# Staggered start addresses for the split activation tiles of a two-layer decoder trunk

## The chip, the cores and the metric

The kernel runs on one core of one Trainium2 chip. The metric is the device time of one launch in microseconds (us), median of the runs. A difference is told in us and in per cent of that median.

## What is computed

Two layers on 512 tokens of width 1024, in float32. Each is a mixer between an input and an output projection, then a LayerNorm of the residual and a gated addition of a per-layer embedding:

```python
def reference(x, p, ...):
    for i in range(DEPTH):                      # 2
        if i % 2 == 0:
            s = conv_gdn_mixer(x, w_in_even[j], ...)   # 1024 -> 8208, short conv and gated delta rule, 2048 -> 1024
        else:
            s = hgrn2_mixer(x, w_in_odd[j], ...)       # 1024 -> 8192, gated linear recurrence, 2048 -> 1024
        x = layer_norm(DEEPNORM_ALPHA * x + s, ln_g[i], ln_b[i])
        gate = jax.nn.sigmoid((x @ w_pl_gate[i]).astype(jnp.float32))
        x = x + ((p[i] @ w_pl[i]).astype(jnp.float32) * gate).astype(x.dtype)
    return x
```

Five large products make up most of the work: the two input projections, the two output projections and the gate products, all over 128-deep slices of the contraction.

## The kernel before, in words

**The split.** Every float32 operand of a large product is kept as two tiles of a rounded 32-bit type: a high half (`xh`, `yh`, `x1h`, `ph`, `whi`) and a low half (`xl`, `yl`, `x1l`, `pl`, `wlo`). ScalarE writes the high half (L104, L160), VectorE the low one (L105, L161). `mm3` (L107 to L114) then makes three matmuls of each 128-deep slice: high weight with high activation (L112), high weight with low activation (L113), low weight with high activation (L114). Transposes and the recurrences use plain float32 matmuls instead.

**The tiles.** The layer's input x, transposed, lies in 16 tiles of 128 partitions by 512 columns (2048 bytes in each partition): `xh0` to `xh7` and `xl0` to `xl7`, made in `load_x` from the pool `acts` and kept for both layers. The mixer's output lies in 32 such tiles, `yh0` to `yh15` and `yl0` to `yl15` (`open_y`, a pool at the right end of the memory). After the LayerNorm each half of the tokens has 16 tiles of 256 columns, `x1h` and `x1l` (`x1tiles`; the first half in the pool of the tail, the second in the pool of the gates). A weight chunk is one tile pair of 128 by 1024, eight slices of 128 columns (512 bytes) each, in three buffers (`chunk_tiles`).

**Where they begin.** Take the offset of a tile to be its start address in the partition, less the last multiple of 512. Before the change, every weight slice has offset 448, every `xh` and `xl` offset 0, every `yh`, `yl`, `x1h`, `x1l`, `ph` and `pl` offset 384, and nearly all other working tiles of the two layers offset 384 (a few of the odd layer 352). Three small tiles that nothing reads (`ytop`, `askew`, `sskew`) set these offsets. The small weights of the two gate columns, `wba_h` and `wba_l` (128 by 16 for each slice), begin at 448 and go on by 64 bytes from slice to slice.

**The order.** `proj` runs eight slices of one weight chunk against the eight `xh` and `xl` pairs: 24 matmuls of 512 columns into one accumulator. `out_proj` runs 16 slices against `yh` and `yl`, for four of the eight output blocks with 512 columns and for four with 256 columns, twice. `hgrn_values` (accumulator `pi`) has it the other way round: there slices of `xh` and `xl` are the stationary operand and the weight tiles the moving one, in 256 columns. The gate products (`product`, accumulator `pgate`) run 256 columns of `x1h` and `x1l`. Between slices `pump` lets the steps of the recurrences in, by counts written out at the top of the file (GD, HG, LN). All DMAs are issued from the SyncE queue.

In the profile a matmul row names output<-moving operand and weight: `pq<-xh,whi` streams `xh` through the array against `whi`.

Of the kernel before, what the change touches and what calls it, by code (L numbers as in the profile page):

```python
# [14 lines left out]
F32 = mybir.dt.float32  # L15
F32R = mybir.dt.float32r
# [6 lines left out]
P = 128  # L23
D = 1024
KD = D // P
S = 512
# [21 lines left out]
class K:  # L48
# [110 lines left out]
    def split_to(self, hi, lo, src):  # L159
        self.nc.scalar.copy(hi, src)  # L160
        self.nc.vector.tensor_tensor(lo, src, hi.bitcast(F32), op=SUB)  # L161


    def constants(self):
        nc, cp = self.nc, self.const
# [96 lines left out]
    def load_x(self, srcs):  # L262

        nc = self.nc
        self.xh = [self.acts.tile([P, S], F32R, name=f"xh{k}") for k in range(KD)]
        self.xl = [self.acts.tile([P, S], F32R, name=f"xl{k}") for k in range(KD)]
        chs = [self.chunk_tiles() for _ in srcs]
        with self.tc.tile_pool(name="xin", bufs=1, reuse_waits="tile") as xp:
            for k in range(KD):
                if k % 2 == 0:  # L270
                    self.chunk_part(chs[0], srcs[0], slice(k * P, (k + 2) * P))
                raw = xp.tile([P, S], F32, name=f"xraw{k}")
                nc.sync.dma_start(raw, self.a["xT"][:, k * S:(k + 1) * S])
                self.split_to(self.xh[k], self.xl[k], raw)
                if k % 2 == 0:
                    for ch, src in zip(chs[1:], srcs[1:]):
                        self.chunk_part(ch, src, slice(k * P, (k + 2) * P))
        pss = [self.acc("pqkv") for _ in srcs]
        for k in range(KD):
            for ps, (_, hi, lo) in zip(pss, chs):  # L280
                self.mm3(ps, [(hi[:, k, :], lo[:, k, :], self.xh[k], self.xl[k])], k == 0, k == KD - 1)
        self.pre = pss

    def open_y(self, layer):
        self.ystack = ExitStack()
        yp = self.ystack.enter_context(
            self.tc.tile_pool(name=f"y{layer}", bufs=1, side="right", reuse_waits="tile"))
        self.yh = [yp.tile([P, S], F32R, name=f"yh{k}") for k in range(2 * KD)]
        self.yl = [yp.tile([P, S], F32R, name=f"yl{k}") for k in range(2 * KD)]


    def gates(self, hp):
# [610 lines left out]
    def tail(self, layer, wout, last):  # L903
        nc, a = self.nc, self.a
        NH = 2
        HT = S // NH
        sm = self.smalls
        tp = self.tc.tile_pool
        with tp(name=f"tail{layer}", bufs=1, reuse_waits="tile") as lp, self.psum(f"pt{layer}") as self.ps:
# [38 lines left out]
                self.split_to(ph.rearrange("p a b -> p (a b)"), pl_.rearrange("p a b -> p (a b)"), praw)  # L948

            def x1tiles(pool, hf):  # L950
                return [(pool.tile([P, HT], F32R, name=f"x1h{hf}_{f}"),
                         pool.tile([P, HT], F32R, name=f"x1l{hf}_{f}")) for f in range(KD)]

            def norm_half(hf):
                hs = slice(hf * HT, (hf + 1) * HT)
# [28 lines left out]
            self.prio = PRIO  # L984
            load_p()
            x1[0] = x1tiles(lp, 0)
            self.start(0, norm_half(0))
            out_proj((5, 6, 7), HT, HT, held)
# [3 lines left out]
            self.ystack.close()  # L992
            with tp(name=f"gate{layer}", bufs=1, side="right", reuse_waits="tile") as gp:
                x1[1] = x1tiles(gp, 1)
                self.start(0, norm_half(1))

# [123 lines left out]
```

## Time and profile before

| | us |
|---|---|
| median of 3 runs | 1229.6 |
| lowest and highest of them | 1228.88, 1230.12 |
| the profiled execution's own time | 1228.3 |
| its span, first to last instruction | 1226.6 |
| TensorE busy in it | 1208.9 |
| VectorE, ScalarE, GpSimd busy | 805.9, 560.1, 45.9 |

The profile is of one execution. TensorE's busy time is the union of its matmuls' spans, and these overlap, since a matmul's record runs on until its last result is out. How fast a stretch of matmuls runs is therefore read from start to start, not from the length of a record: the start of the last of n+1 matmuls in a row less the start of the first, divided by n. This is called the pace below.

### The profile page before, as it was taken

The numbers are of one execution on the slowest core, as the hardware profiler recorded it, in microseconds if no ns is written. First come the engines' busy times: TensorE is split into PE (matmuls) and PEld (weight loads), VectorE is DVE, ScalarE is ACT, GpSimd is POOL, SyncE is SP. The second block draws the span as 40 slices with busy tenths as digits, with TensorE's granted clock in tenths as the row PEclk, the third lists the DMA queues.
The fourth block names the chain that finished last, engine by engine and source line by source line (L and its number), as shares of the span: only waits on it lengthen the run. The fifth ranks groups of instructions, "written<-read, shape, count | busy, mean of one in ns | idle before, by whom it ended". The sixth has DMA issues, their size and how long they took to land.

```text
span 1226.6 us, 23658 instructions
## 1 busy us (share of the span) xinstructions
PE 1208.9 (99%) x9590; PEld 1025.3 (84%) x9590; DVE 805.9 (66%) x1835; ACT 560.1 (46%) x1316; POOL 45.9 (4%) x75
## 2 busy tenths in 40 slices
PE   7999999999999999999999999999999999999998
PEld 5777878787787788898998888888888888889988
DVE  7678777776869754349856475665757575644884
ACT  5554645354545443237534444443535444433471
POOL 3000000000000000111000000000000000001100
PEclk9999999999999999999999999999999999999999
DMA  6223222232222223354442221222122222234432
GB/s 212 85 75 102 69 87 87 73 100 70 87 82 90 62 78 99 112 160 131 153 136 88 72 77 62 87 69 88 57 96 73 78 79 69 87 103 152 142 102 88
DMA packets 37309, 117.07 MB, mean 95 GB/s; under 512 B 4144, under 2 KB 8016, under 8 KB 37200
## 3 DMA queue, kind: packets, MB, share of 16 engines
q1 hardware_dynamic: 37200, 115.56, 29.5%
q8 instruction: 75, 1.23, 0.4%
q14 instruction: 34, 0.28, 0.1%
HBM read 111.32 MB, written 4.23 MB: 94 GB/s over the span
## 4 chain that ended last, share of the span: by engine, by line
PE 85%; DVE 9%; ACT 4%; issue 1%; DMA 0%; POOL 0%; SPq 0%; DVEq 0%; POOLq 0%; ACTq 0%
PE pz L112 5%; PE pz L113 5%; PE pz L114 5%; PE pout L112 4%; PE pout L114 4%; PE pout L113 4%; PE pqkv L113 3%; PE pqkv L114 3%; PE pqkv L112 3%; PE pf L112 3%; PE pq L112 2%; PE pf L114 2%; PE pf L113 2%; PE pq L114 2%; PE pq L113 2%; PE pgate L113 2%
## 5 line engine op out<-in xcount | busy, mean ns | idle before, releaser
L104 ACT CAST whi<-wraw 128x1024 fp32r<-128x1024 f32 (+1 forms) x196 | 200.7, 1024 | 335.5 <-PE pout L113 87.0
L105 DVE TENSOR_TENSOR wlo<-wraw,whi 128x1024 fp32r<-128x1024 f32 (+1 forms) x196 | 238.5, 1217 | 168.1 <-ACT whi L104 167.4
L112 PE MATMUL pout<-yh,whi 128*128 128x256 f32 (+1 forms) x384 | 122.7, 320 | 0.0
L114 PE MATMUL pout<-yh,wlo 128*128 128x256 f32 (+1 forms) x384 | 122.5, 319 | 0.0
L113 PE MATMUL pout<-yl,whi 128*128 128x256 f32 (+1 forms) x384 | 122.0, 318 | 0.0
L112 PE MATMUL pz<-xh,whi 128*128 128x512 f32 x256 | 104.1, 406 | 0.0
L114 PE MATMUL pz<-xh,wlo 128*128 128x512 f32 x256 | 101.1, 395 | 0.0
L113 PE MATMUL pz<-xl,whi 128*128 128x512 f32 x256 | 100.8, 394 | 0.0
L112 PE MATMUL pqkv<-xh,whi 128*128 128x512 f32 x192 | 79.7, 415 | 4.9 <-ACT xh L160 4.9
L114 PE MATMUL pqkv<-xh,wlo 128*128 128x512 f32 x192 | 77.8, 405 | 2.6 <-DVE wlo L105 2.6
L113 PE MATMUL pqkv<-xl,whi 128*128 128x512 f32 x192 | 78.9, 411 | 0.0
L112 PEld LDWEIGHTS pout<-yh,whi 128*128 128x128 f32 x384 | 72.6, 189 | 5.8
L114 PEld LDWEIGHTS pout<-yh,wlo 128*128 128x128 f32 x384 | 72.4, 188 | 5.6
L113 PEld LDWEIGHTS pout<-yl,whi 128*128 128x128 f32 x384 | 72.2, 188 | 5.6
L112 PE MATMUL pi<-whi,xh 128*128 128x256 f32 x256 | 72.6, 284 | 0.0
L113 PE MATMUL pi<-wlo,xh 128*128 128x256 f32 x256 | 72.0, 281 | 0.0
L113 PE MATMUL pgate<-x1l,whi 128*128 128x256 f32 x256 | 71.2, 280 | 0.4 <-DVE x1l L161 0.4
L114 PE MATMUL pi<-whi,xl 128*128 128x256 f32 x256 | 71.2, 278 | 0.0
L112 PE MATMUL pgate<-x1h,whi 128*128 128x256 f32 x256 | 70.7, 281 | 0.1
L114 PE MATMUL pgate<-x1h,wlo 128*128 128x256 f32 x256 | 70.7, 278 | 0.0
L114 PEld LDWEIGHTS pz<-xh,wlo 128*128 128x128 f32 x256 | 48.1, 188 | 10.4
L112 PEld LDWEIGHTS pz<-xh,whi 128*128 128x128 f32 x256 | 48.2, 188 | 9.6
(326 smaller groups left out, 2876.4 us busy)
## 6 DMA issues: line engine op xcount, KB each, us to landing
wraw<-in_we SPq DMA_DIRECT2D x62, 512.0 KB, 3.5
wraw<-in_wo SPq DMA_DIRECT2D x48, 512.0 KB, 3.5
wraw<-in_woe SPq DMA_DIRECT2D x21, 512.0 KB, 3.5
wraw<-in_woo SPq DMA_DIRECT2D x21, 512.0 KB, 3.4
wraw<-in_wg SPq DMA_DIRECT2D x16, 512.0 KB, 3.7
wraw<-in_wi SPq DMA_DIRECT2D x16, 512.0 KB, 3.5
gb<-drows SPq DMA_DIRECT2D x8, 512.0 KB, 3.8
xraw<-in_xT SPq DMA_DIRECT2D x8, 256.0 KB, 4.5
```

The lines of the kernel that those rows point to most:

```text
L104: nc.scalar.copy(hi, raw)
L105: nc.vector.tensor_tensor(lo, raw, hi.bitcast(F32), op=SUB)
L112: nc.tensor.matmul(ps, wh, xh, start=first and i == 0, stop=False)
L113: nc.tensor.matmul(ps, wh, xl, start=False, stop=False)
L114: nc.tensor.matmul(ps, wl, xh, start=False, stop=last and i == n - 1)
```

## The change

A helper `skewed` makes a list of tiles with a spacer of 16 floats (64 bytes) behind each, so that each tile of the list begins 64 bytes further within 512 than the one before. `load_x`, `open_y` and `x1tiles` take their high tiles from it, then a spacer of 8 floats (32 bytes), then their low tiles. Nothing writes or reads the spacers. The scratch that the program reserves for DMA descriptors made in software is halved, from 16384 to 8192 bytes in each partition, which makes room.

| tiles | offset before | offset after |
|---|---|---|
| weight slices `whi`, `wlo` | 448 | 448 |
| `xh0`, `xh1`, ... `xh7` | 0 | 0, 64, ... 448 |
| `xl0`, `xl1`, ... `xl7` | 0 | 32, 96, ... 480 |
| `yh0`, `yh1`, `yh2`, `yh3`, ... | 384 | 352, 416, 480, 32, ... |
| `yl0`, `yl1`, `yl2`, ... | 384 | 384, 448, 0, ... |
| `x1h` and `x1l`, first half | 384 | from 416 and from 448, by 64 |
| `x1h` and `x1l`, second half | 384 | from 352 and from 384, by 64 |
| `ph`, `pl` | 384 | 416 |
| other working tiles of the two layers | 384 (few 352) | 416 (few 384; some of the tail 448) |

No instruction is added, removed or moved: on each engine the built programs have the same operations on the same tiles in the same order, and each waits for the same semaphore values. The addresses alone differ.

```diff
+    def skewed(self, pool, n, names):
+
+        tiles = []
+        for name in names:
+            tiles.append(pool.tile([P, n], F32R, name=name))
+            pool.tile([P, 16], F32, name=name + "_s")
+        return tiles
...
-        self.xh = [self.acts.tile([P, S], F32R, name=f"xh{k}") for k in range(KD)]
-        self.xl = [self.acts.tile([P, S], F32R, name=f"xl{k}") for k in range(KD)]
+        self.xh = self.skewed(self.acts, S, [f"xh{k}" for k in range(KD)])
+        self.acts.tile([P, 8], F32, name="xskew")
+        self.xl = self.skewed(self.acts, S, [f"xl{k}" for k in range(KD)])
...
-        self.yh = [yp.tile([P, S], F32R, name=f"yh{k}") for k in range(2 * KD)]
-        self.yl = [yp.tile([P, S], F32R, name=f"yl{k}") for k in range(2 * KD)]
+        self.yh = self.skewed(yp, S, [f"yh{k}" for k in range(2 * KD)])
+        yp.tile([P, 8], F32, name="yskew")
+        self.yl = self.skewed(yp, S, [f"yl{k}" for k in range(2 * KD)])
...
-                return [(pool.tile([P, HT], F32R, name=f"x1h{hf}_{f}"),
-                         pool.tile([P, HT], F32R, name=f"x1l{hf}_{f}")) for f in range(KD)]
+                xh = self.skewed(pool, HT, [f"x1h{hf}_{f}" for f in range(KD)])
+                pool.tile([P, 8], F32, name=f"x1skew{hf}")
+                return list(zip(xh, self.skewed(pool, HT, [f"x1l{hf}_{f}" for f in range(KD)])))
...
-    nc = _bacc.Bacc("TRN2", target_bir_lowering=False, num_devices=1)
+    nc = _bacc.Bacc("TRN2", target_bir_lowering=False, num_devices=1, dynamic_dma_scratch_size=8192)
```

## Rows read from the trace of the kernel before

**Rows 1.** The page: TensorE's busy time, and the chain that ended last.
```profile
PE 1208.9 (99%) x9590; PEld 1025.3 (84%) x9590; DVE 805.9 (66%) x1835; ACT 560.1 (46%) x1316; POOL 45.9 (4%) x75
...
PE 85%; DVE 9%; ACT 4%; issue 1%; DMA 0%; POOL 0%; SPq 0%; DVEq 0%; POOLq 0%; ACTq 0%
```

**Rows 2.** TensorE's groups by shape: count | busy us, mean ns | idle before.
```profile
L112 PE MATMUL pz<-xh,whi 128*128 128x512 f32 x256 | 104.1, 406 | 0.0
...
L112 PE MATMUL pi<-whi,xh 128*128 128x256 f32 x256 | 72.6, 284 | 0.0
...
L112 PE MATMUL pout<-yh,whi 128*128 128x256 f32 x256 | 71.7, 280 | 0.0
...
L112 PE MATMUL pgate<-x1h,whi 128*128 128x256 f32 x256 | 70.7, 281 | 0.1
...
L112 PE MATMUL pout<-yh,whi 128*128 128x512 f32 x128 | 51.0, 400 | 0.0
...
L112 PE MATMUL pc<-xh,whi 128*128 128x512 f32 x64 | 27.0, 421 | 0.0
...
L112 PE MATMUL ppl<-ph,whi 128*128 128x512 f32 x32 | 13.0, 408 | 0.0
```

**Rows 3.** Timeline of TensorE, second layer: start us, length us, instruction; 32 in a row.
```profile
1029.70 0.39 PE L113 MATMUL pq<-xl,whi 128*128 128x512 f32 x1
...
1036.80 0.39 PE L114 MATMUL pq<-xh,wlo 128*128 128x512 f32 x1
```

**Rows 4.** The same in the second output projection, 54 in a row.
```profile
1083.63 0.39 PE L113 MATMUL pout<-yl,whi 128*128 128x512 f32 x1
...
1095.99 0.40 PE L112 MATMUL pout<-yh,whi 128*128 128x512 f32 x1
```

**Rows 5.** The same near the start: 5 in a row, then 34 in a row.
```profile
23.94 0.63 PE L114 MATMUL pqkv<-xh,wlo 128*128 128x512 f32 x1
...
25.64 0.63 PE L112 MATMUL pqkv<-xh,whi 128*128 128x512 f32 x1
...
26.35 0.40 PE L114 MATMUL pqkv<-xh,wlo 128*128 128x512 f32 x1
...
34.05 0.39 PE L114 MATMUL pz<-xh,wlo 128*128 128x512 f32 x1
```

**Rows 6.** The gate columns right behind them: 24 in a row, and the next.
```profile
34.28 0.39 PE L112 MATMUL ba<-xh,wba_h 128*16 128x512 f32 x1
...
39.83 0.40 PE L112 MATMUL pqkv<-xh,whi 128*128 128x512 f32 x1
```

**Rows 7.** Gate products of the first layer, 55 in a row, and of the second, 54.
```profile
599.80 0.28 PE L112 MATMUL pgate<-x1h,whi 128*128 128x256 f32 x1
...
605.92 0.28 PE L112 MATMUL pgate<-x1h,whi 128*128 128x256 f32 x1
...
1206.74 0.28 PE L112 MATMUL pgate<-x1h,whi 128*128 128x256 f32 x1
...
1212.98 0.28 PE L114 MATMUL pgate<-x1h,wlo 128*128 128x256 f32 x1
```

**Rows 8.** Stretches: length, busy us (count) of each engine, PEclk, DMA share, GB/s.
```profile
24.00:25.60 1.60, 1.60 (x5) 1.28 (x4) 1.60 (x4) 0.07 (x1) 0.00 (x0) 0.50 0.85 210
26.40:34.00 7.60, 7.60 (x34) 6.18 (x33) 6.01 (x9) 3.47 (x5) 0.00 (x0) 1.00 0.50 172
...
600.00:605.90 5.90, 5.90 (x54) 5.90 (x53) 5.90 (x9) 3.69 (x5) 0.95 (x1) 1.00 0.65 220
1207.00:1213.00 6.00, 6.00 (x54) 6.00 (x53) 3.17 (x5) 0.60 (x1) 0.00 (x0) 1.00 0.13 46
```

**Rows 9.** VectorE writing the state `S`: count: ns min/median/max, when, shape.
```profile
L858 DVE SCALAR_TENSOR_TENSOR S<-S,T,dS x32: 340/344/348, 687.9 to 1073.6; 128x128 f32<-128x128 f32 x32
L518 DVE SCALAR_TENSOR_TENSOR S<-S,eg,dS x16: 341/344/348, 98.7 to 463.5; 128x128 f32<-128x128 f32 x16
```

**Rows 10.** The page: DMA queues.
```profile
q1 hardware_dynamic: 37200, 115.56, 29.5%
```

## The prediction

> **What bounds the kernel now.** I read the page first: TensorE is busy for 1208.9 of the span's 1226.6 us, and the chain of work that ended last runs through TensorE for 85% of the span, VectorE for 9%, ScalarE for 4% [rows 1]. So time is gained or lost where matmuls take longer or shorter, and on most of the span it comes through. The built programs hold the same instructions in the same order with the same waits; all that the change can touch is how long an instruction takes at another address.
>
> The groups by shape count the matmuls that read a moved tile; each group is there three times, for the lines L112 to L114 [rows 2]. Matmuls of 512 columns that stream `xh` or `xl`: six groups from `pz` (256) to `pc` (64), which with the others of their kind (the 64 chunks of the first layer and 48 of the second, 24 matmuls each) make 2688, and 24 more for the gate columns: 2712. Of 512 columns on `yh`, `yl`, `ph`, `pl`: 3 x (128 + 32) = 480. Of 256 columns (`pi`, `pout`, `pgate`): 3 x (256 + 256 + 256) = 2304.
>
> The timeline then gives the pace, from start to start. `xh` at offset 0 in the second layer: (1036.80 - 1029.70) / 31 = 229.0 ns [rows 3]. `yh` at offset 384: (1095.99 - 1083.63) / 53 = 233.2 ns [rows 4]. So equal shapes go at two paces at one clock. But an offset does not settle it: right behind the start the same `xh` at the same offset 0 goes at (34.05 - 26.35) / 33 = 233.3 ns [rows 5], and the gate products, the same lines on the same offsets in both layers, go at 6.12 / 54 = 113.3 ns in the first and 6.24 / 53 = 117.7 ns in the second [rows 7]. Each pace holds for a long run of matmuls.
>
> What chooses the pace? Not the clock: it is granted in full (1.00, the 2.4 GHz level) in all those stretches [rows 8]. Not the neighbours: the quicker gate stretch has VectorE busy throughout and DMAs at 220 GB/s, the slower one VectorE half busy and 46 GB/s [rows 8]. So it lies within TensorE, in how its stream of moving columns and its weight loads stand to each other, and it locks: with equal offsets from matmul to matmul, a relation once reached repeats. One stretch shows the lock broken. In the gate columns the weights go on by 64 bytes from slice to slice, while `xh` stays; there the pace is (39.83 - 34.28) / 24 = 231.2 ns [rows 6], between the two; behind it the 229.0 pace begins and 233.3 is gone. That is the nearest row to the changed kernel, where the moving tile goes on by 64 bytes from slice to slice and the weights stay.
>
> **The change part by part.**
>
> 1. `xh` and `xl` staggered, 2712 matmuls, priced at 229.0 now [rows 3]. Below, the cost is bounded by that pace itself (0) and by the other pace seen on the same tiles, 233.3 [rows 5]: 2712 x 4.3 ns = 11.7 us. I take the broken lock, 231.2 [rows 6], since it is the only row with offsets that change from slice to slice: 2712 x 2.2 ns = **+6.0 us**.
>
> 2. `yh` and `yl` staggered, `ph` and `pl` shifted, 480 matmuls, priced at 233.2 now [rows 4]. Between 229.0 (480 x -4.2 ns = -2.0 us) and the 233.3 of today (0). I take 231.2 again: 480 x -2.0 ns = **-1.0 us**.
>
> 3. 256 columns, 2304 matmuls: `x1h`, `x1l` and `yh`, `yl` staggered as moving operands, `xh`, `xl` as weights in `pi`. Today both paces occur, 113.3 and 117.7 [rows 7]; I price today's mixture at the middle, 115.5, and the broken lock there too: **0**, between -5.1 us (2304 x -2.2 ns, all at 113.3) and +5.1 us (all at 117.7).
>
> 4. Everything else that moved by 32 bytes (offset 384 to 416). No row has these tiles at 416, but the odd layer's `S` lies at 352, also 32 away from a multiple of 64, and the even layer's at 384, and VectorE's update of it takes 344 ns in the median in both [rows 9]. I take 0 for VectorE and ScalarE, and a loss there is covered twice: VectorE is on 9% of the chain. The plain float32 matmuls read the same kinds of tiles at half the rate of columns; I take 0.
>
> 5. The halved scratch. The data goes through one queue whose descriptors hardware makes, 115.56 MB [rows 10]; the scratch is for the other kind. 0. Should it be read after all, a DMA would start late at the weight chunks, and the matmuls that use them would wait.
>
> The sum on the matmuls is 6.0 - 1.0 + 0 = 5.0 us. In the parts of the span where VectorE or ScalarE leads, slower matmuls eat slack; with TensorE's 85% of the chain 4.3 us arrive, with all of it 5.0. On the profiled execution's own 1228.3 us that is 1232.6. The median is 1229.6, 1.3 us above it, so I forecast 1229.6 + 4.3 = 1233.9, rounded to **1234 us**, with 1230 to 1239 as this case's own range.
>
> **The rivals.**
>
> The quick pace everywhere (chance 0.23). If the stagger keeps the weight load out of the stream's way in all relations, step 1 is 0, step 2 is -2.0 and step 3 -5.1: -7.1 us, of which 85% is -6.0: **1223.6 us**. For it speaks that 229.0 and 113.3 are what most stretches find by themselves; against it, that the one staggered stretch was not at 229.
>
> The slow pace everywhere (0.12). 11.7 + 0 + 5.1 = 16.8 us, 85% of it 14.3: **1243.9 us**. That happens if each relation on the way through 512 bytes meets the bad one often enough to be held up once in every matmul. For it: all of `yh` at 384 is at 233.2 in 54 matmuls without an exception; against it: the 231.2. Should the stagger add one more step of 4.3 ns (6.6 per 256 columns over the middle), 40.6 us follow, 85% of it 34.5: 1264 (0.04).
>
> Nothing (0.14). The change then doesn't do what it says: where a tile begins doesn't matter, the lock comes from the order of matmul and weight load alone, and both paces return as often as before: **1229.6 us**. For it: the same offsets have both paces. Against it: `yh` never left 233.2, and two offsets with one pace each, 0 with 229.0 and 384 with 233.2, would be chance [rows 3, 4]. The Trainium skill says the same from its side ("SBUF — State Buffer", Who interferes with whom): TensorE has two independent read ports, one for the moving operand and one for the weights, and "PE and ACT never wait on anyone". By that rule the sum is 0. The trace doesn't agree outright: [rows 7] show 113.3 and 117.7 at one shape, one clock and the same offsets, so something in TensorE does wait.
>
> A larger gain (0.09). At half the clock (0.50, the 1.2 GHz level [rows 8]) 512 columns took 1.70 / 4 = 425 ns [rows 5]; half of it, 213, is what the full clock would give if nothing were lost, so 16 ns of each 229.0 are lost at the full clock. If the loss comes from streams and loads that begin in the same place within 512, and the stagger ends it, 2712 x 16 + 480 x 20 + 2304 x 9 ns = 74 us are to be had, 85% of it 63: **1167 us**, and any part of it. Against it: the gate columns, staggered, with weights of only 16 columns to load, still lose 18. The figure of the Trainium skill ("TensorE: Matmul & The Clock Gate", Back-to-back issue gap) is 2.5 ns over the columns' own time for a lone matmul, and would put nearly all of this loss down to something that can be avoided.
>
> **How the numbers follow.** The forecast has 0.38, the quick pace 0.23, nothing 0.14, the slow pace 0.12, the larger gain 0.09, the extra step 0.04. The range leaves out the larger gain, the extra step and some of the ends: **1218 to 1245 us**. A measurement of this kernel can tell about 0.2%, 2.5 us, from no change. Slower by more: 0.30 of the forecast, the slow pace and the extra step, 0.46. Within: 0.06 of the forecast and nothing, 0.20. Faster: 0.02 of the forecast, the quick pace and the larger gain, 0.34.
>
> **What would show it.** In the changed kernel's timeline, stretches of `pq` near 231 ns, `pout` of 512 columns near 231, the gate products near 115 in both layers: each step right. `pq` at 229.0 and `pout` at 233.2 again: nothing. `pq` at 226 or below: a larger gain, and the forecast is wrong in sign. `pq` at 233 and above in all stretches: the slow pace. If VectorE's 344 ns or ScalarE's casts moved, step 4 is wrong; if the pace is right but the time is not, the 85% is.

## The result and the profile after

The changed kernel takes 1235.3 us (median of 4 runs, 1234.9 to 1236.5) against 1229.2 us (1227.6 to 1230.1) of the kernel before beside it: the ratio is 1.0062, with an interval from 1.0047 to 1.0077. The change makes the kernel slower by about 0.6%: 7.6 us by the ratio (5.8 to 9.5), 6.1 us between the two medians.

The page of the changed kernel, engines' busy time and then the chain that ended last; the lines of before are [rows 1]:

```profile
PE 1217.2 (99%) x9590; PEld 1030.9 (84%) x9590; DVE 805.6 (65%) x1835; ACT 559.7 (45%) x1316; POOL 45.6 (4%) x75
...
PE 91%; DVE 5%; ACT 1%; issue 1%; DMA 0%; POOL 0%; SPq 0%; DVEq 0%; POOLq 0%
```

The counts are the same on every engine. TensorE is busy for 8.3 us more (1217.2 less 1208.9), VectorE, ScalarE and GpSimd within 0.4 us of what they were, and the chain has gone over from VectorE and ScalarE (13% before, 6% now) to TensorE. So the matmuls have become slower, and nothing else has in a way that shows.

Which matmuls, the timeline tells; start in us, length in us, engine, line, instruction. First `xh` and `xl`, at the start of the kernel (23 in a row) and in the second layer (40 in a row):

```profile
28.15 0.40 PE L113 MATMUL pz<-xl,whi 128*128 128x512 f32 x1
...
33.24 0.40 PE L114 MATMUL pz<-xh,wlo 128*128 128x512 f32 x1
...
1033.80 0.39 PE L114 MATMUL pq<-xh,wlo 128*128 128x512 f32 x1
...
1042.82 0.39 PE L114 MATMUL pq<-xh,wlo 128*128 128x512 f32 x1
```

The paces are 5.09 / 22 = 231.4 ns and 9.02 / 39 = 231.3 ns, where [rows 5] had 233.3 and [rows 3] 229.0. There is one pace for `x` now, between the two. Then `yh` and `yl` of 512 columns in the second output projection, 54 in a row:

```profile
1090.62 0.39 PE L113 MATMUL pout<-yl,whi 128*128 128x512 f32 x1
...
1102.94 0.40 PE L112 MATMUL pout<-yh,whi 128*128 128x512 f32 x1
```

12.32 / 53 = 232.5 ns, after 233.2 in [rows 4]: quicker by little. Last the products of 256 columns, in order of time: the gates of the first layer (61 in a row), `pi` (39 in a row) and the gates of the second layer (57 in a row):

```profile
604.81 0.28 PE L113 MATMUL pgate<-x1l,whi 128*128 128x256 f32 x1
...
611.92 0.28 PE L113 MATMUL pgate<-x1l,whi 128*128 128x256 f32 x1
...
988.16 0.28 PE L113 MATMUL pi<-wlo,xh 128*128 128x256 f32 x1
...
992.66 0.28 PE L112 MATMUL pi<-whi,xh 128*128 128x256 f32 x1
...
1213.34 0.28 PE L112 MATMUL pgate<-x1h,whi 128*128 128x256 f32 x1
...
1219.94 0.28 PE L114 MATMUL pgate<-x1h,wlo 128*128 128x256 f32 x1
```

7.11 / 60 = 118.5, 4.50 / 38 = 118.4 and 6.60 / 56 = 117.9 ns. The quick 113.3 of the first layer in [rows 7] is gone, and `pi` has lost as much; here it is in the kernel before, also 39 in a row, 4.32 / 38 = 113.7 ns:

```profile
983.28 0.28 PE L113 MATMUL pi<-wlo,xh 128*128 128x256 f32 x1
...
987.60 0.28 PE L112 MATMUL pi<-whi,xh 128*128 128x256 f32 x1
```

**The account.** Both programs have the same matmuls in the same order, so each step, from the start of one matmul to the start of the next, can be set against the same step of the other trace. The first 34 us have to be taken by themselves. From 22.8 to 26.2 us TensorE's granted clock was 0.50, the 1.2 GHz level, in the trace of before, and 1.00, the 2.4 GHz level, in that of the changed kernel. The length, the busy us (count) of each engine, PEclk, DMA share and GB/s of that stretch, before and then after:

```profile
22.80:26.20 3.40, 3.40 (x10) 2.66 (x9) 3.40 (x8) 1.04 (x1) 0.00 (x0) 0.50 0.80 206
...
22.80:26.20 3.40, 3.40 (x17) 2.75 (x15) 3.40 (x10) 1.22 (x2) 0.00 (x0) 1.00 0.63 184
```

In the 12 us up to 22 us TensorE had been busy for 9.4 us in the first trace and 9.9 us in the second. The slow stretch does not follow the addresses: of the traces below, those of e3, e6 and e7 have one as well, those of e1, e2, e4, e8 and e9 have none. The gate columns begin at 34.28 us before [rows 6] and 0.81 us earlier after; the last matmul of before and then the first gate column and the last matmul of after:

```profile
1222.17 0.28 PE L114 MATMUL pgate<-x1h,wlo 128*128 128x256 f32 x1
...
33.47 0.39 PE L112 MATMUL ba<-xh,wba_h 128*16 128x512 f32 x1
...
1228.82 0.28 PE L114 MATMUL pgate<-x1h,wlo 128*128 128x256 f32 x1
```

From the first gate column to the last matmul the changed kernel takes 1195.35 us and the kernel before 1187.89, so 7.5 us more; the span rose by 6.6 (1233.2 less 1226.6). The steps between products of the split that are steady in both traces (up to 245 ns for 512 columns, 126 ns for 256) take 3.8 us more in 512 columns (2633 steps) and 6.6 in 256 (2236), 10.4 in all. All other steps, those held up for longer and those of the plain float32 matmuls, take 2.9 us less. That fits a TensorE that waits there for other engines, which are as quick as before; it is argued from the sums and not shown wait by wait.

### The profile page after: what moved, and what is told of

Its sections match the earlier page's. It is cut to its first block, busy times and chain, and to the rows that moved or that the text cites. A ratio compares the mean times of both kernels' runs of the same rounds, so it can differ in the third digit from the quotient of the medians.

```text
span 1233.2 us, 23658 instructions
## 1 busy us (share of the span) xinstructions
PE 1217.2 (99%) x9590; PEld 1030.9 (84%) x9590; DVE 805.6 (65%) x1835; ACT 559.7 (45%) x1316; POOL 45.6 (4%) x75
## 4 chain that ended last, share of the span: by engine, by line
PE 91%; DVE 5%; ACT 1%; issue 1%; DMA 0%; POOL 0%; SPq 0%; DVEq 0%; POOLq 0%
PE pz L112 5%; PE pz L114 5%; PE pz L113 5%; PE pout L114 4%; PE pout L112 4%; PE pout L113 4%; PE pqkv L113 3%; PE pqkv L114 3%; PE pqkv L112 3%; PE pi L112 3%; PE pi L113 3%; PE pf L112 3%; PE pi L114 2%; PE pq L113 2%; PE pf L113 2%; PE pq L112 2%
```

## The experiments

Four theories stand behind the expectations. **A**, that of the prediction: stream and weight load lock, and offsets that change from slice to slice break the lock; any stagger gives 231. **B**: the moving tile's own offset sets its pace. **C**: the offset plays no part. **D**: what counts is the distance from the start of the moving tile to the start of the weight slice; it took its form, the distance modulo 256 bytes, from the streams of the fifth experiment. All kernels but that one, which leaves the decoder out, have the instructions, the order and the waits of the kernel before; the addresses alone differ.

This table holds the mean paces of all steady matmuls in each trace, in ns (first layer / second layer where they differ), and the ratio of the time to the kernel before of the same session with its interval.

| kernel | `x`, 512 | `pout` on `y`, 512 | `pout`, 256 | `pgate`, 256 | `pi`, 256 | ratio |
|---|---|---|---|---|---|---|
| before | 229.6 | 233.4 | 115.4 | 113.5 / 117.0 | 114.9 | 1 |
| after | 231.4 | 232.4 | 118.0 | 118.1 / 118.0 | 118.3 | 1.0062 [1.0047, 1.0077] |
| e1_x_only | 231.4 | 233.3 | 114.2 / 114.6 | 113.6 / 113.8 | 118.3 | 1.0041 [1.0028, 1.0053] |
| e2_x1_only | 229.5 | 233.4 | 115.4 | 117.8 / 117.7 | 114.4 | 1.0017 [1.0008, 1.0026] |
| e6_y_only | 229.5 | 232.4 | 118.0 | 113.7 / 113.6 | 115.0 | 1.0012 [1.0003, 1.0021] |
| e3_x_at_384 | 233.3 | 233.4 | 114.2 / 115.4 | 113.6 / 113.8 | 117.3 | 1.0062 [1.0048, 1.0076] |
| e4_all_at_0 | 229.9 / 229.5 | 229.0 | 117.8 | 117.8 / 117.7 | 114.9 | 1.0006 [0.9997, 1.0015] |
| e8_x_at_192 | 228.9 / 228.0 | 233.3 | 113.4 / 114.6 | 113.8 / 113.9 | 119.9 | 0.9992 [0.9978, 1.0005] |
| e9_step_256 | 229.4 / 229.6 | 233.4 | 115.4 | 114.4 / 113.6 | 114.6 | 0.9997 [0.9986, 1.0008] |
| e7_matched | 228.3 / 228.0 | 227.1 | 117.1 / 115.8 | 117.4 / 117.0 | 115.3 | 0.9967 [0.9955, 0.9979] |

### The parts of the change, one at a time

**The stagger of `xh` and `xl` alone** (e1), with a spacer that leaves all other tiles where they were modulo 512:

```
+        self.xh = self.skewed(self.acts, S, [f"xh{k}" for k in range(KD)])
+        self.acts.tile([P, 8], F32, name="xskew")
+        self.xl = self.skewed(self.acts, S, [f"xl{k}" for k in range(KD)])
```

> Only xh and xl are staggered; yh, yl, x1h, x1l and all working tiles keep their offset 384. Theory A (a lock between the stream of columns and the weight loads, broken when offsets change from slice to slice): 512 columns on xh, xl at 231.4 ns as in the changed kernel, pi (xh, xl as weights) near 118; yh at 233.3; the gate products at either of their paces. Time: 2712 x 1.9 + 768 x 3.4 ns = 7.7 us on the matmuls, about half of which arrives as it did with the whole change: +3 to +5 us. Theory B (each tile has the pace of its own offset, 0 being the good one): the same for xh, and pi unchanged at 115, since a stationary tile at another offset has no pace of its own: +2 to +4 us.

**The stagger of `x1h` and `x1l` alone** (e2):

```
+                xh = self.skewed(pool, HT, [f"x1h{hf}_{f}" for f in range(KD)])
+                pool.tile([P, 8], F32, name=f"x1skew{hf}")
+                return list(zip(xh, self.skewed(pool, HT, [f"x1l{hf}_{f}" for f in range(KD)])))
```

> Only x1h and x1l are staggered. Both theories: gate products at 118.0 in both layers in place of 113.3 and 117.8, so 768 x 2.7 ns = 2.1 us on the matmuls, nearly all of it in the first layer. Theory A expects starts that no longer repeat; theory B expects the pace of the offset 384 for no tile but the first ones. Time: +1 to +2 us. Everything else as before.

**The stagger of `yh` and `yl` alone** (e6):

```
+        self.yh = self.skewed(yp, S, [f"yh{k}" for k in range(2 * KD)])
+        yp.tile([P, 8], F32, name="yskew")
+        self.yl = self.skewed(yp, S, [f"yl{k}" for k in range(2 * KD)])
```

> Only yh and yl are staggered. Both theories: 512 columns on yh at 232.4 in place of 233.3, 256 columns on yh at 118.0 in place of 115.4, all else as before: 384 x -0.9 + 768 x 2.6 ns = +1.7 us on the matmuls. These stretches have little of VectorE and ScalarE on the chain, so nearly all of it arrives: +1 to +2 us. If the parts add up, the whole change's 6.1 us is e1 (4.9) + e2 (1.8) + this, so this one would have to be near 0.

They measure 1.0041, 1.0017 and 1.0012: 5.0, 2.1 and 1.5 us on some 1228, together 8.6, which is within the interval of the whole (5.8 to 9.5 us). So the parts account for the change as far as the intervals tell, each part slows the kernel down, and in each it is the matmuls that read the moved tile, as weights too: with `x` alone moved, `pi`, for which `xh` and `xl` are the weights, goes from 114.9 to 118.3. By the prediction's terms the parts cost +6.0, 0 and -0.8 us on the matmuls.

### One fixed offset for all

**`xh` and `xl` all at 384, without a stagger** (e3; the tiles behind them keep their offsets modulo 512):

```
-        self.acts.tile([P, 16], F32, name="askew")
+        self.acts.tile([P, 112], F32, name="askew")
```

> No stagger: all xh and xl at offset 384 in place of 0, all other tiles where they were. Theory A: one offset for all slices keeps the lock, so the starts repeat; at which pace it locks is open (229.0 or 233.3). Theory B: 512 columns on xh, xl at 233.3, as yh at 384 has it: 2712 x 3.7 ns = 10 us on the matmuls, +5 to +9 us. A rival C (the offset plays no part at all): 229.6 on average as before, time within 1 us of before.

The timeline of this kernel in the second layer, 39 in a row, 8.87 / 38 = 233.4 ns:

```profile
1036.03 0.39 PE L113 MATMUL pq<-xl,whi 128*128 128x512 f32 x1
...
1044.90 0.39 PE L112 MATMUL pq<-xh,whi 128*128 128x512 f32 x1
```

The pace of [rows 4] now holds for `x`, in both layers, with nothing else moved. That is the end of C, and the time is as long as that of the whole change.

**The converse: `y`, `x1`, `ph` and the working tiles from 384 to 0** (e4):

```
-        pool("ytop", 1, side="right").tile([P, 24], F32, name="ytop")
+        pool("ytop", 1, side="right").tile([P, 120], F32, name="ytop")
...
-        self.small.tile([P, 16], F32, name="sskew", bufs=1)
+        self.small.tile([P, 48], F32, name="sskew", bufs=1)
```

> No stagger: yh, yl, x1h, x1l, ph, pl and the working tiles at offset 0 in place of 384; xh, xl stay at 0. Theory B: 512 columns on yh at 229.0 in place of 233.3 (480 x -4.3 ns = -2.1 us), and the 256-column products at the quick 113.3 more often (up to 1536 x -2 ns = -3 us): time -1 to -4 us. Theory A: locked at some pace, 229.0 or 233.3, both layers alike. Rival C (the offset plays no part): yh at 233.3 and time as before.

The gates of the first layer (155 in a row) and `pout` of 512 columns in the second (78 in a row):

```profile
596.78 0.28 PE L112 MATMUL pgate<-x1h,whi 128*128 128x256 f32 x1
...
614.92 0.28 PE L113 MATMUL pgate<-x1l,whi 128*128 128x256 f32 x1
...
1082.24 0.40 PE L113 MATMUL pout<-yl,whi 128*128 128x512 f32 x1
...
1099.87 0.39 PE L112 MATMUL pout<-yh,whi 128*128 128x512 f32 x1
```

18.14 / 154 = 117.8 ns and 17.63 / 77 = 229.0 ns. At offset 0 the 512 columns win 4.4 ns and the 256 columns, on the same tiles and the same weights, lose: of these two offsets neither is good for both. By the table the 480 matmuls win 2.1 us, `pout` and `pgate` of 256 columns lose 1.8 and 1.9, and the time is no different from before (1.0006, 0.9997 to 1.0015), where theory B had a gain.

### The streams by themselves

This kernel (e5) leaves the decoder out and ran once. It has groups of 48 equal matmuls on fixed data, with the weight slices at offset 448, and does all groups twice, the second time in reverse. `coa` to `cop` stream 512 columns with the moving tiles at offset 0, 32, ... 480, `cqa` to `cqp` 256 columns, groups that begin with p stream the weights past slices of the activations (as `pi` does), and others have staggered tiles. Its heart:

```
+            for i in range(48):
+                r, k, m = i // 24, i // 3 % 8, i % 3
+                w0 = 128 * k + fw(k) // 4
+                x0 = 512 * k + (fl(k) if m == 1 else fh(k)) // 4
...
+                    st, mv = (wl if m == 2 else wh)[:, w0:w0 + P], (xl if m == 1 else xh)[:, x0:x0 + n]
+                nc.tensor.matmul(ps[:, :n], st, mv, start=i == 0, stop=i == 47)
```

> The decoder is left out: this kernel only streams. Groups of 48 matmuls in the kernel's pattern (high, low, high; eight slices, twice), each group with one rule for the offsets and each run twice, in opposite orders: `co` 512 columns with one offset for all tiles, letters a to p for 0, 32, ... 480, weights at 448; `cq` the same with 256 columns; `sfull` and `tfull` (512 and 256 columns) the offsets of the changed kernel; `ssame`, `tsame` the stagger by 64 with high and low at equal offsets; `slow`, `tlow` high at 0 and low at 32, no stagger; `swgt`, `twgt` the weights staggered by 64 in place of the activations; `sboth`, `tboth` both staggered, so that their difference stays; `p` with 256 columns of weights streaming against slices of the activation tile, at one offset or staggered. Theory B (each tile has the pace of its own offset): `coa` 229.0, `com` (384) 233.3, and sfull near the mean of all sixteen `co` groups; swgt equal to coa; sboth equal to ssame. Theory A (broken lock): the `co` groups at 229 or 233, sfull 231.4 whatever their mean is, swgt at 231 too, and sboth back at a locked 229 or 233. For 256 columns the same with 113.3 and 117.8; tfull at 118.0.

The timeline, from the 4th to the 48th matmul of a group, 44 steps: moving tiles at 192 (`cog`), at 384 (`com`) and at 0 (`coa`, second pass), then 256 columns at 0 (`cqa`) and at 128 (`cqe`), and 512 columns with the stagger of the change (`sfull`):

```profile
96.16 0.39 PE L1107 MATMUL cog<-xh,wh 128*128 128x512 f32 x1
...
106.15 0.39 PE L1107 MATMUL cog<-xh,wl 128*128 128x512 f32 x1
...
168.89 0.40 PE L1107 MATMUL com<-xh,wh 128*128 128x512 f32 x1
...
179.16 0.39 PE L1107 MATMUL com<-xh,wl 128*128 128x512 f32 x1
...
217.02 0.28 PE L1107 MATMUL cqa<-xh,wh 128*128 128x256 f32 x1
...
222.20 0.28 PE L1107 MATMUL cqa<-xh,wl 128*128 128x256 f32 x1
...
243.97 0.28 PE L1107 MATMUL cqe<-xh,wh 128*128 128x256 f32 x1
...
248.96 0.28 PE L1107 MATMUL cqe<-xh,wl 128*128 128x256 f32 x1
...
634.83 0.39 PE L1107 MATMUL sfull<-xh,wh 128*128 128x512 f32 x1
...
645.00 0.40 PE L1107 MATMUL sfull<-xh,wl 128*128 128x512 f32 x1
...
936.41 0.40 PE L1107 MATMUL coa<-xh,wh 128*128 128x512 f32 x1
...
946.49 0.40 PE L1107 MATMUL coa<-xh,wl 128*128 128x512 f32 x1
```

227.0, 233.4, 117.7, 113.4, 231.1 and 229.1 ns. Over the 16 offsets the paces repeat after 256 bytes. Here they are by the distance, start of the weight slice less start of the moving tile, modulo 256, as means of those 44 steps over both passes and both offsets (without the first pass of `coa`, whose first matmuls went at 426 ns):

| distance | 0 | 32 | 64 | 96 | 128 | 160 | 192 | 224 |
|---|---|---|---|---|---|---|---|---|
| 512 columns, ns | 227.2 | 233.2 | 233.4 | 234.2 | 233.1 | 233.3 | 229.0 | 233.3 |
| 256 columns, ns | 119.8 | 118.3 | 113.4 | 117.4 | 118.7 | 120.0 | 117.8 | 116.7 |
| 256 columns, weights streaming | 119.8 | | 113.5 | | 118.7 | | 117.8 | |

The third line has the weights streaming from 448 and the activations as slices at 192, 0, 64 and 128 (and 256 more), and its distance is the slice's start less that of the streaming weights. The offsets of the two operands have changed places there, and it agrees with the second line only when both are read by their difference. So B falls too, as its own test has it (weights alone staggered, 231.5 ns, where B had the 229.0 of `coa`): what counts is how far the two starts lie apart. And the best distance for 256 columns (64) is among the bad ones for 512.

### D tested in the kernel

**Weights put at distance 0 from what they meet** (e7). The weight tiles become 1088 wide (so some of their buffers begin at 192 and not at 448, which is the same modulo 256), and a chunk is written 16 floats further in for the `x` products (448 + 64 - 0 = 512) and 48 further for the 512-column products on `y`, `ph` and `pl` (448 + 192 - 384 = 256); for 256 columns it stays:

```
+        hi = self.wp.tile([P, 1088], F32R, tag="whi", name="whi", bufs=3)
...
+        return raw, hi[:, o:o + 1024], lo[:, o:o + 1024]
...
-        hi, lo = self.chunk(src)
+        hi, lo = self.chunk(src, 16)
...
-                            chunks.append(self.chunk(wout[2 * f + kh]))
+                            chunks.append(self.chunk(wout[2 * f + kh], 48 if n == S else 0))
```

> Theory D, formed on the streams of e5: the pace goes by the distance from the start of the moving tile to the start of the weight slice that is loaded meanwhile, modulo 256 bytes. For 512 columns 0 is best (227.3 ns), for 256 columns 64 (113.3). Activations stay where before has them; the weight tiles get 64 spare columns, and each chunk is put at the distance that suits its use: +64 bytes for the products of xh and xl, +192 for yh, yl, ph, pl with 512 columns, +0 for all products with 256 columns. Expected: pq at 227.3 in place of 229.0, pout of 512 columns and ppl at 227.3 in place of 233.3, all else as before; 2688 x -2.2 and 480 x -6.1 ns = -8.8 us on the matmuls, of which 55 to 85% arrive: -5 to -7.5 us. Theory B (only the moving tile's own offset counts) expects no change, since the activations didn't move.

The second layer's `pq` (41 in a row) and `pout` of 512 columns (76 in a row):

```profile
1026.38 0.40 PE L113 MATMUL pq<-xl,whi 128*128 128x512 f32 x1
...
1035.45 0.39 PE L114 MATMUL pq<-xh,wlo 128*128 128x512 f32 x1
...
1080.77 0.40 PE L113 MATMUL pout<-yl,whi 128*128 128x512 f32 x1
...
1097.79 0.39 PE L113 MATMUL pout<-yl,whi 128*128 128x512 f32 x1
```

9.07 / 40 = 226.8 and 17.02 / 75 = 226.9 ns: the pace of `cog`, where [rows 3] and [rows 4] had 229.0 and 233.2, though no activation has moved. By the table's means the `x` products win 2712 x 1.4 = 3.9 us, the other 480 some 2.7, and the 256 columns lose about 2.5. The time is 1223.0 us against 1227.6, a ratio of 0.9967 (0.9955 to 0.9979), 4.1 us less by the ratio. This version is quicker than both kernels, but by less than the 5 to 7.5 us expected: `x` stayed at 228.3 and 228.0 in the mean, `ppl` at 229.3 in place of 227.3, and the 256 columns were slower. Its trace is of an execution of 1226.8 us, the second longest of twelve, so the paces in the table are those of a slow execution, and that the gain comes from the matmuls is read from paces and not from this trace's span.

**`xh` and `xl` at 192** (e8), distance 0 for them as moving tiles, and 0 for `pi` as well, where 0 is bad:

```
-        self.acts.tile([P, 16], F32, name="askew")
+        self.acts.tile([P, 64], F32, name="askew")
```

> No stagger; all xh and xl at offset 192 in place of 0, weights at 448, all else as before. Theory D: 512 columns on xh at distance 0, so 227.3 in place of 229.6 (2712 x -2.3 = -6.2 us), and pi, where xh and xl are the weights, near 119.8 in place of 114.9 (768 x 4.9 = +3.8 us): -2.4 us on the matmuls, -1 to -2 us in time. Theory A (a lock at some pace for any equal offsets): 229.0 or 233.3. Theory B (0 is the good offset): 233.3 and +5 to +8 us.

`pq` of the second layer, 41 in a row:

```profile
1026.86 0.39 PE L113 MATMUL pq<-xl,whi 128*128 128x512 f32 x1
...
1035.95 0.39 PE L114 MATMUL pq<-xh,wlo 128*128 128x512 f32 x1
```

`pq` goes at 9.09 / 40 = 227.3 ns, and `pi`, by the table, at 119.9: `x` gains (some 3 us over 2712, by the layers' means), `pi` gives back (768 x 5.0 ns = 3.8 us), as the two lines of the distance table have it. The time is that of before.

**A stagger in steps of 256 bytes** (e9), `xh` and `xl` at 0, 256, 0, 256, ...:

```
+            tiles.append(pool.tile([P, n], F32R, name=name))
+            pool.tile([P, 64], F32, name=name + "_s")
```

> xh and xl staggered, but by 256 bytes from tile to tile in place of 64 (offsets 0 and 256 in turn, high and low alike); all else at before's offsets. Theory D: the distance modulo 256 doesn't change, so 229.0 on xh, pi as before, and time as before within 1.5 us. Theory A (any change of the offset from slice to slice breaks the lock): 231.4 on xh and +3 to +5 us, as in e1.

Timeline, 41 in a row:

```profile
1026.61 0.40 PE L113 MATMUL pq<-xl,whi 128*128 128x512 f32 x1
...
1035.78 0.39 PE L114 MATMUL pq<-xh,wlo 128*128 128x512 f32 x1
```

9.17 / 40 = 229.3 ns, [rows 3] again, and the time is the same (0.9986 to 1.0008). Offsets that change from slice to slice cost nothing in themselves, as long as they change by the period. With that A, too, falls as a mechanism. (The scratch is halved in this kernel, so that costs nothing either.)

## Why the prediction was right, and where it was not

The forecast was 1234 us, the median came out at 1235.3, and the sign and the range held. But the difference of 4.3 us lies below the interval of the ratio (5.8 to 9.5), the steps did not all hold, and the reason given for the pace was in part wrong.

- **What bounds.** Right. Only the matmuls moved: from the gate columns on, the steady ones alone lost 10.4 us, more than the 7.5 us that the trace became longer there. The 6.6 us of span hold 0.8 us that the changed kernel's trace gained in the first 34 us, where that of before has its stretch at half the clock.
- **Step 1, `xh` and `xl`, +6.0.** Right in the pace, 231.4 where the row of the gate columns [rows 6] gave 231.2, though the reason is a mean over distances and not a broken lock (below). In the mean over all steady matmuls today's pace was 229.6, not 229.0, so the term measures 2712 x 1.85 ns = 5.0 us.
- **Step 2, `yh`, `yl`, `ph`, `pl`, -1.0.** Right in sign, half the size: 233.4 to 232.4 for `pout`, 0.5 for `ppl`, some -0.4 us.
- **Step 3, 256 columns, 0.** This is the step that failed. I had set both today's mixture and the broken lock at the middle of 113.3 and 117.7. Today's mixture is 115.4, 115.3 and 114.9 in the mean; the staggered products are at 118.0 to 118.3, at or above the upper bound. 768 x (2.6 + 2.7 + 3.4) ns = 6.7 us where I had 0, over the bound of +5.1. There was no row with 256 staggered columns, and I put my value in the middle instead of asking what would keep the quick pace; `pi` I priced without a row of its own at all.
- **Steps 4 and 5, 0.** Right. VectorE's update of `S`, count, then least, median and greatest ns, in the changed kernel:

```profile
L868 DVE SCALAR_TENSOR_TENSOR S<-S,T,dS x32: 340/344/348, 691.0 to 1079.2; 128x128 f32<-128x128 f32 x32
L528 DVE SCALAR_TENSOR_TENSOR S<-S,eg,dS x16: 338/342/349, 98.1 to 463.9; 128x128 f32<-128x128 f32 x16
```

  It is what [rows 9] show, and the scratch is cleared by the last experiment.
- **85% arrives.** Of the 10.4 us that the steady steps lost from the gate columns on, 7.5 arrived, 72%; the ratio's 7.6 us are 73% of it, with an interval that reaches past 85%. The traces show where the rest goes (the other steps got 2.9 us shorter); the exact share stays open. The steps measure 5.0 - 0.4 + 6.7 = 11.3 us on the matmuls where the forecast had 5.0, more than twice as much. The missing 6.7 us of step 3 and the smaller share worked against each other, and that the time fits better than the steps is luck.

**The rivals.** The quick pace everywhere did not come, since the stagger leads every tile past the bad distances: none of the groups that it moved is at its quick pace. The slow pace everywhere came for the 256 columns only. Nothing, 0.14, is out by the ratio and by C's fall. The "larger gain" had hold of something: there is time in the relation of stream and load, but the quickest of the distances gives 227 ns, not 213, so some 4 us and not 63 (e7), and a stagger is the wrong way to it. The Trainium skill ("SBUF — State Buffer", Who interferes with whom) says that TensorE waits on no one at this memory; by that rule an offset would change nothing. The runs do not agree: 229.6 became 233.3 by moving `x` alone, and 228.2 in the mean (226.8 in the 41 shown) by moving the weights. What they show is not TensorE waiting for another engine, but its own two operands that do not go independently of each other. The Trainium skill's other figure ("TensorE: Matmul & The Clock Gate", Back-to-back issue gap), 2.5 ns over the columns' own time for a lone matmul, no run here shows; the quickest stream lost 227.2 less 213, 14 ns.

**What the mechanism is.** The lock was half of it: a fixed relation does give a fixed pace in most stretches. But it was the relation's size that mattered, not that it stays. Staggered tiles take all distances in turn, and the pace is then near their mean. From the distance table, with the high tile counted twice (it meets `whi` and `wlo`): `x` has high tiles at distances 192, 128, 64, 0 and low ones at 160, 96, 32, 224, so (2 x (229.0 + 233.1 + 233.4 + 227.2) + 233.3 + 234.2 + 233.2 + 233.3) / 12 = 231.6 ns; measured, 231.4. `y` has it the other way round, (2 x 934.0 + 922.7) / 12 = 232.6; measured, 232.4. `pout` and `pgate` of 256 columns likewise 117.9; measured, 118.0. `pi` 117.7; measured, 118.3. A broken lock, at one pace whatever the distances, would not tell `x` from `y`. The rule holds to about 1 ns and no better: in the streams the stagger by 64 with high and low at equal offsets (`ssame`, `tsame`) went at 231.7 and 118.4 where the means are 230.7 and 117.4, high at 0 with low at 32 (`slow`, `tlow`) at 231.2 and 118.3 where they are 230.4 and 118.5, and `tfull` at 117.2, not the 118.0 expected. The means lie above the best and above today's because most distances are bad, six of eight for 512 columns.

**The row that misled.** That "an offset does not settle it" was read from [rows 5] and [rows 7]. The 233.3 of [rows 5] belongs to that one execution. In the traces of e2, e4, e6 and e9, which leave `x` at distance 192, the stretch from 28 to 32 us goes at 228.7 to 228.9, in e6 behind a stretch at half the clock too. In e2, 23 in a row, 5.04 / 22 = 229.1 ns:

```profile
27.04 0.39 PE L113 MATMUL pz<-xl,whi 128*128 128x512 f32 x1
...
32.08 0.40 PE L114 MATMUL pz<-xh,wlo 128*128 128x512 f32 x1
```

**What stays open.** Why it is the distance, and why it repeats after 256 bytes, no run tells; I know that it is so for rounded float32 operands with 128 x 128 weights. In the streams, a stagger of weights and moving tiles together by 64 bytes keeps the distance at 192 and yet went at 230.7, not 229.0 (`sboth`); with 256 columns (`tboth`) it went at 116.8 in the first pass and 113.9 in the second, not 117.8. Weights alone staggered went at 231.5 and 118.3, where the means are 230.7 and 117.4. So something small, about 1 to 4 ns either way, comes on top when the weights move from slice to slice. Nor does distance explain why the products of 256 columns at distance 64 go at 113.4 in most stretches and at 117 in some, without any change of address: `pgate` in the second layer goes at 117.0 in before and at 113.6 to 113.9 in the five experiments of the table that leave it alone without touching the weights. This second pace can move the time by up to 384 x 3.5 = 1.3 us in one layer's gates, so differences of that size between the experiments prove little. In the trace of e7 the 256 columns were mostly at the slower pace, and whether its wider weight tiles did that, or the execution that was traced, was not tried. Nor was the shift of `ph` and `pl` tried by itself.

## What to carry to other kernels

Before you stagger or align tiles, find how the two operands of a matmul stand to each other: list the pace from start to start by shape and by the difference of the two start addresses, since one address alone explains nothing. Where one distance is good, keep it in every matmul rather than vary it, and where shapes want different distances, move the weights for each, as they are written anew for every chunk anyhow. When a term has no row of its own in the trace, as `pi` had none, take a row for it before giving it a zero; two errors that cancel make a good time and a poor lesson.

## What the runs showed of the hardware

- In the streams (e5), matmuls of 512 columns of rounded float32 went at 227.2 to 234.2 ns, and of 256 columns at 113.4 to 120.0 ns, by the distance of weight slice and moving tile modulo 256 bytes. The best distance was 0 for the one and 64 for the other.
- It makes no difference which of the two lies where: in 256 columns, weights at 448 with a moving tile at 128 went at 113.3 and 113.4 ns, and stationary slices at 0 or 256 with the moving tile at 448 at 113.3 to 113.7.
- At distance 64 products of 256 columns have two paces, 113.3 and 117.7 ns in [rows 7], each for a long run of matmuls, with the same addresses. What chooses between them was not found.
- TensorE's granted clock fell to 0.50, the 1.2 GHz level, for 3.4 us near the start in four of ten traces of the decoder (before, e3, e6, e7), whatever the addresses; 512 columns then took 425 ns [rows 5].
